# A hybrid decoder layer on one core: the scheduler's other model of the engines puts the same program in order

## The chip, the cores and the metric

The kernel runs on one core of a Trainium2 chip. The metric is the device time of one execution in microseconds (us), as the median of several runs. The engines of the core are TensorE (PE in the profile, its weight loads PEld), VectorE (DVE), ScalarE (ACT), GpSimd (POOL) and SyncE (SP, which only issues DMAs here).

## The reference

One decoder layer on 512 tokens of width 1024, in float32 (cut to what matters):

```python
h = rms_norm(x, ln_mix_g)
q_a, kv_a, gate_a, q_b, k_b, v_b, r_b, alpha_b, merge = split(h @ w_in)
o_nsa = nsa_attention(...)   # 8 heads, 2 key heads: compressed, selected and window attention, gated
o_gla = gla(...)             # 4 heads of chunked gated linear attention, chunks of 64
mix = sigmoid(merge_1) * (o_nsa @ w_branch_nsa) + sigmoid(merge_2) * (o_gla @ w_branch_gla)
x = x + mix @ w_out
x = x + memory_cross_attention(rms_norm(x, ln_x_g), rms_norm(mem, ln_mem_g), ...)  # 256 memory tokens
x = x + conv_ffn(rms_norm(x, ln_ffn_g), w_up, conv_w, conv_b, w_down)              # width 2816
out = rms_norm(x, ln_final_g)
```

## The kernel before

**Arithmetic.** Activations lie transposed: 128 channels on the partitions, 512 tokens along the row. Every matrix product is made of three fast matmuls (`mm3`, L160 to L162; `dense_tok`, L197 to L199), because each operand is split in a high and a low part: ACT copies the high part (`wh`, L140), and DVE or POOL subtracts it from the raw value to get the low part (`wl`, L141; `lo_engine` says which of the two, and it is POOL during the attention stage).

**Weights.** All weights come as 141 blocks of 128x1024 float32 in the order in which the program takes them (`take`). SP loads a block into one of three `raw` buffers (L126), ACT and DVE or POOL split it into one of three `wh` and `wl` buffers, two blocks ahead of use. A dense product (`dense8`) uses up one block in 24 matmuls.

**Stages.** After a first stage of projections comes the sparse attention (names that begin with `nsa`): eight steps, two key heads times four blocks of 128 queries. In a step `nsa_scores` multiplies on PE (L562 to L594, into the three `sc` banks), DVE masks and takes maxima (L584, L596), ACT exponentiates (L612), DVE, ACT and POOL scale, and DVE weights the compressed part (L627); then `nsa_values` transposes on PE (L650, into the two `pt` banks), ACT and DVE split the result (L165, L166), PE multiplies with the values into the one `o` bank (L644), and ACT and DVE take that out (L664, L669). The gated linear attention follows (`gla`), in which L746 and L791 make states and scores, L791 to L823 outputs and L833 a sum of squares. Between these steps the program holds independent dense products (`fillers`, names with `fill`), whose place is written by hand:

```python
NSA_FILL = (2, 1, 2, 1, 1, 2, 0, 0)
...
    for kv in range(2):
        for i in range(4):
            cur = nsa_scores(kv, i)
            if prev is not None:
                nsa_values(*prev)
            prev = cur
            fill(NSA_FILL[kv * 4 + i])
```

After that come the merge, the output projection, the cross-attention, the up and down projections of the feed-forward part, and a tail that norms the last rows and stores them.

**What sets the order.** The program text fixes which engine runs each instruction, but not the final order on it. When the `tile.TileContext` closes, the Tile library plays the whole program against a model of the engines. Whenever an engine of that model can take an instruction, it gets, among its instructions whose inputs are finished and whose buffers are free, the one that was written first. What comes out is the fixed order of every engine's instructions (the queue of SP among them), the buffer that each tile gets, and with both the waits on semaphores. On the chip each engine then works through its list in that order and waits at the head of it.

## Time and profile before

| | |
|---|---|
| median of 3 runs | 873.84 us (873.72 to 873.98) |
| the profiled execution, device time | 875.57 us |
| its span, first to last instruction | 873.5 us |
| PE busy | 853.2 us, 98% of the span, 4174 matmuls |
| DVE, ACT, POOL busy | 557.7, 419.1, 214.2 us |
| DMA | 83.58 MB, 96 GB/s in the mean |

The span is what the views of the trace divide up; 2.1 us of the device time lie outside it. Matmuls overlap one another in the records, so a record is longer than the distance to the next one's start, and PE can be busy and still not be at its pace. Bracketed times in a timeline row are the idle time of that engine just before the instruction, with what ended it.

### The profile page before, as it was taken

The numbers are of one execution on the slowest core, as the hardware profiler recorded it, in microseconds if no ns is written. First come the engines' busy times: TensorE is split into PE (matmuls) and PEld (weight loads), VectorE is DVE, ScalarE is ACT, GpSimd is POOL, SyncE is SP. The second block draws the span as 40 slices with busy tenths as digits, with TensorE's granted clock in tenths as the row PEclk, the third lists the DMA queues.
The fourth block names the chain that finished last, engine by engine and source line by source line (L and its number), as shares of the span: only waits on it lengthen the run. The fifth ranks groups of instructions, "written<-read, shape, count | busy, mean of one in ns | idle before, by whom it ended". The sixth has DMA issues, their size and how long they took to land.

```text
span 873.5 us, 11086 instructions
## 1 busy us (share of the span) xinstructions
PE 853.2 (98%) x4174; PEld 708.0 (81%) x4174; DVE 557.7 (64%) x908; ACT 419.1 (48%) x731; POOL 214.2 (25%) x160
## 2 busy tenths in 40 slices
PE   9999989999998999999999999999999999999996
PEld 6987777777786878898888788888888888888996
DVE  7576977998858378454487669665533465565324
ACT  7466767798445455344446535433311233334311
POOL 1373444344333314112300222111100111112121
PEclk9999999999999999999999999999999999999999
DMA  8333221002221232244341132322222223222302
GB/s 293 116 123 97 73 73 49 25 2 73 67 78 49 96 116 103 96 169 146 123 143 49 48 121 74 120 96 97 97 97 96 97 86 108 90 97 102 121 25 97
DMA packets 26406, 83.58 MB, mean 96 GB/s; under 512 B 3056, under 2 KB 5104, under 8 KB 26352
## 3 DMA queue, kind: packets, MB, share of 16 engines
q1 hardware_dynamic: 26064, 82.58, 27.2%
q8 instruction: 33, 0.54, 0.3%
q10 hardware_dynamic: 288, 0.28, 0.1%
q14 instruction: 21, 0.17, 0.1%
HBM read 80.76 MB, written 2.10 MB: 95 GB/s over the span
## 4 chain that ended last, share of the span: by engine, by line
PE 88%; DVE 7%; ACT 3%; issue 1%; POOL 1%; ACTq 0%; POOLq 0%
PE up_ps_sc L161 4%; PE up_ps_sc L160 4%; PE up_ps_sc L162 4%; PE fill_ps_acc L160 3%; PE fill_ps_acc L161 3%; PE fill_ps_acc L162 3%; PE up_ps_pt L160 3%; PE up_ps_pt L161 3%; PE up_ps_pt L162 3%; PE up_ps_acc L161 2%; PE up_ps_acc L160 2%; PE up_ps_acc L162 2%; PE nsa_ps_o L644 2%; PE down_ps_sc L162 2%; PE nsa_ps_pt L650 2%; PE down_ps_sc L161 2%
## 5 line engine op out<-in xcount | busy, mean ns | idle before, releaser
L1068 POOL TENSOR_TENSOR up_s<-up_s,up_s 128x512 f32<-128x512 f32 x22 | 35.8, 1630 | 259.6 <-ACT up_wh L140 207.7
L140 ACT ACTIVATE up_wh<-up_raw 128x1024 fp32r<-128x1024 f32 x40 | 42.5, 1062 | 64.9 <-PE up_ps_sc L161 33.0
L141 DVE TENSOR_TENSOR up_wl<-up_raw,up_wh 128x1024 fp32r<-128x1024 f32 x40 | 62.8, 1569 | 16.0 <-ACT up_wh L140 15.9
L141 POOL TENSOR_TENSOR fill_wl<-fill_raw,fill_wh 128x1024 fp32r<-128x1024 f32 x16 | 38.5, 2407 | 48.7 <-ACT fill_wh L140 46.7
L160 PE MATMUL up_ps_sc<-xo_g,up_wh 128*128 128x512 f32 x124 | 48.7, 393 | 0.0
L162 PE MATMUL up_ps_sc<-xo_g,up_wl 128*128 128x512 f32 x124 | 48.3, 389 | 0.0
L161 PE MATMUL up_ps_sc<-xo_g,up_wh 128*128 128x512 f32 x124 | 48.3, 389 | 0.0
L160 PE MATMUL up_ps_pt<-xo_g,up_wh 128*128 128x512 f32 x104 | 40.6, 390 | 0.0
L162 PE MATMUL up_ps_pt<-xo_g,up_wl 128*128 128x512 f32 x104 | 40.5, 389 | 0.0
L161 PE MATMUL up_ps_pt<-xo_g,up_wh 128*128 128x512 f32 x104 | 40.5, 389 | 0.0
L612 ACT ACTIVATE nsa_s<-nsa_s,nsa_nm 128x128 f32<-128x128 f32 (+3 forms) x64 | 34.2, 536 | 11.7 <-DVE nsa_nm L603 11.7
L160 PE MATMUL fill_ps_acc<-in_g,fill_wh 128*128 128x512 f32 x96 | 38.3, 399 | 0.2 <-DVE fill_t L529 0.2
L161 PE MATMUL fill_ps_acc<-in_g,fill_wh 128*128 128x512 f32 x96 | 38.3, 399 | 0.0
L162 PE MATMUL fill_ps_acc<-in_g,fill_wl 128*128 128x512 f32 x96 | 38.1, 396 | 0.0
L162 PE MATMUL up_ps_acc<-xo_g,up_wl 128*128 128x512 f32 x88 | 34.2, 389 | 0.0
L161 PE MATMUL up_ps_acc<-xo_g,up_wh 128*128 128x512 f32 x88 | 34.2, 389 | 0.0
L160 PE MATMUL up_ps_acc<-xo_g,up_wh 128*128 128x512 f32 x88 | 34.2, 389 | 0.0
L1064 ACT ACTIVATE up_s<-up_s 128x512 f32<-128x512 f32 x22 | 13.8, 632 | 40.2 <-DVE up_s L1062 40.2
L140 ACT ACTIVATE down_wh<-down_raw 128x1024 fp32r<-128x1024 f32 x9 | 9.5, 1061 | 39.4 <-PE down_ps_sc L161 17.5
L224 POOL TENSOR_TENSOR xo_g<-xo_g,xo_t 128x512 f32<-128x512 f32 x7 | 12.3, 1756 | 63.8 <-ACT xo_g L214 61.3
L140 ACT ACTIVATE fill_wh<-fill_raw 128x1024 fp32r<-128x1024 f32 x16 | 16.9, 1057 | 21.9 <-PE fill_ps_acc L161 14.9
L160 PEld LDWEIGHTS up_ps_sc<-xo_g,up_wh 128*128 128x128 f32 x124 | 23.3, 188 | 5.1 <-issue 0.2
(943 smaller groups left out, 2716.0 us busy)
## 6 DMA issues: line engine op xcount, KB each, us to landing
up_raw<-in_w SPq DMA_DIRECT2D x44, 512.0 KB, 3.2
fill_raw<-in_w SPq DMA_DIRECT2D x20, 512.0 KB, 3.2
down_raw<-in_w SPq DMA_DIRECT2D x18, 512.0 KB, 3.2
proj_raw<-in_w SPq DMA_DIRECT2D x14, 512.0 KB, 3.3
mix_raw<-in_w SPq DMA_DIRECT2D x12, 512.0 KB, 3.3
mkv_raw<-in_w SPq DMA_DIRECT2D x8, 512.0 KB, 3.2
wout_raw<-in_w SPq DMA_DIRECT2D x8, 512.0 KB, 3.4
in_s<-in_xT SPq DMA_DIRECT2D x8, 256.0 KB, 5.4
```

The costliest lines, as they stand in the source:

```text
L140: nc.scalar.activation(wh[:, c], r[:, c], AF.Copy)
L141: lo.tensor_tensor(wl[:, c], r[:, c], wh[:, c].bitcast(F32), op=ALU.subtract)
L160: nc.tensor.matmul(ps, w[0], x[0], start=first, stop=False)
L161: nc.tensor.matmul(ps, w[0], x[1], start=False, stop=False)
L162: nc.tensor.matmul(ps, w[1], x[0], start=False, stop=last)
L224: eng.tensor_tensor(state[0], state[0], q, op=ALU.add)
L612: nc.scalar.activation(s[:, :w], s[:, :w], AF.Exp, scale=sl, bias=nm[:, c:c + 1], accum_out=sums[:, c:c + 1])
L644: nc.tensor.matmul(po, v, x, start=j == 0 and x is parts[0], stop=j == last and x is parts[-1])
L650: nc.tensor.transpose(pt[:, g * P:(g + 1) * P], srcs[g], C("ident"))
L1064: nc.scalar.activation(cv, cv, AF.Gelu_apprx_tanh)
L1068: nc.gpsimd.tensor_tensor(gm, gm, cv, op=ALU.mult)
```

## The change

One argument is added where the context is opened. It tells the library to play the program against its other model of the engines, a simulation of the whole timeline, when it chooses the order. No instruction is added, taken away or given to another engine by the text of the kernel, and no size, buffer count or hand-written place of a filler changes. What can change is the order of the instructions on each engine and in each DMA queue, which buffer a tile gets, and which waits follow from both.

```diff
-    with tile.TileContext(nc) as tc:
+    with tile.TileContext(nc, schedule_with_timeline_sim=True) as tc:
         layer_kernel(tc, *args, order)
```

## Rows read from the trace of the kernel before

**Rows 1.** The page, busy time of each engine (share of the span, instructions).

```profile
PE 853.2 (98%) x4174; PEld 708.0 (81%) x4174; DVE 557.7 (64%) x908; ACT 419.1 (48%) x731; POOL 214.2 (25%) x160
```

**Rows 2.** Busy time in five stretches: length, engines (instructions), PE clock, DMA share, GB/s.

```profile
40.00:78.00 38.00, 36.76 (x245) 30.60 (x243) 26.72 (x46) 23.08 (x33) 24.62 (x18) 1.00 0.42 139
78.00:222.00 144.00, 136.68 (x691) 107.94 (x691) 118.90 (x337) 108.78 (x267) 60.85 (x52) 0.99 0.14 48
222.00:310.00 88.00, 85.01 (x428) 69.34 (x428) 60.53 (x100) 40.27 (x67) 28.02 (x13) 1.00 0.20 67
310.00:820.00 510.00, 509.88 (x2346) 425.28 (x2347) 306.03 (x360) 206.91 (x296) 80.56 (x51) 1.00 0.31 106
820.00:873.50 53.50, 46.16 (x274) 43.45 (x272) 19.71 (x29) 12.88 (x28) 12.49 (x11) 0.97 0.14 50
```

**Rows 3.** PE's waits, the first of the list: total us, times, longest.

```profile
PE nsa_ps_o L644 <- DVE nsa_t L669: 3.2, 4, 1.9
```

**Rows 4.** Timeline of PE around its six longest waits.

```profile
78.41 0.60 PE L562 MATMUL nsa_ps_sc<-proj_kcmp,proj_g 128*128 128x62 f32 x4 [1.12 <-DVE nsa_mx L596]
78.84 0.47 PE L160 MATMUL fill_ps_acc<-in_g,proj_wh 128*128 128x512 f32 x1
...
111.06 0.47 PE L644 MATMUL nsa_ps_o<-nsa_pth,proj_g 128*128 128x512 f32 x1 [1.92 <-DVE nsa_t L669]
111.37 0.40 PE L162 MATMUL fill_ps_acc<-in_g,fill_wl 128*128 128x512 f32 x1
111.60 0.40 PE L160 MATMUL fill_ps_acc<-in_g,fill_wh 128*128 128x512 f32 x1
...
170.53 0.44 PE L581 MATMUL nsa_ps_sc<-in_pair,proj_g 128*128 128x384 f32 x1 [0.91 <-DVE nsa_mx L584]
...
171.69 0.39 PE L197 MATMUL gla_ps_acc<-fill_wh,in_g 128*128 128x512 f32 x1
...
210.41 0.47 PE L644 MATMUL nsa_ps_o<-nsa_pth,proj_g 128*128 128x512 f32 x1 [0.98 <-ACT gla_s L202]
210.72 0.39 PE L197 MATMUL gla_ps_sc<-gla_wh,in_g 128*128 128x512 f32 x1
...
262.60 0.45 PE L160 MATMUL fill_ps_acc<-in_g,fill_wh 128*128 128x512 f32 x1
263.93 1.12 PE L833 MATMUL gla_ps_pt<-gla_t,in_cst 128*128 128x512 f32 x2 [0.88 <-ACT gla_t L828]
...
266.47 0.73 PE L746 MATMUL gla_ps_sc<-gla_s,gla_t 64*128 64x256 f32 x8 [0.98 <-DVE gla_t L166]
```

**Rows 5.** Timeline of DVE: five long instructions ahead of those waits.

```profile
73.89 2.40 DVE L316 TENSOR_TENSOR proj_g<-proj_t,proj_g 64x512 fp32r<-64x512 f32 x1
...
106.72 2.48 DVE L627 TENSOR_TENSOR proj_cm<-proj_cm,nsa_cf 128x124 f32<-128x124 f32 x1
...
168.37 1.26 DVE L501 COPY fill_dec<-fill_t 128x8 f32<-128x8 f32 x1
...
206.92 2.48 DVE L783 TENSOR_TENSOR gla_g<-fill_g,gla_g 64x512 fp32r<-64x512 f32 x1
...
263.38 2.43 DVE L166 TENSOR_TENSOR gla_g<-gla_t,gla_g 128x512 fp32r<-128x512 f32 x1 [0.41 <-ACT gla_g L165]
```

**Rows 6.** Line L627, all eight: shortest, median and longest in ns.

```profile
L627 DVE TENSOR_TENSOR proj_cm<-proj_cm,nsa_cf x8: 268/273/2475, 86.0 to 202.8; 128x124 f32<-128x124 f32 x8
```

**Rows 7.** Timeline of POOL at the second of them.

```profile
106.63 2.43 POOL L141 TENSOR_TENSOR fill_wl<-fill_raw,fill_wh 128x1024 fp32r<-128x1024 f32 x1
```

**Rows 8.** Busy time in two short stretches around 111 us, columns as in rows 2.

```profile
107.00:110.50 3.50, 2.14 (x11) 1.48 (x10) 3.49 (x7) 1.18 (x3) 2.05 (x1) 1.00 0.12 20
...
112.40:115.90 3.50, 3.50 (x12) 2.81 (x11) 2.18 (x6) 2.74 (x10) 0.39 (x1) 0.51 0.02 5
```

**Rows 9.** PE's matmuls that read `in_g`, 200 to 222.1 us: length, busy (count), clock, DMA.

```profile
200.00:222.10 22.10, 9.99 (x37) 1.00 0.21 74
```

**Rows 10.** Timeline of DVE in the tail.

```profile
857.82 4.88 DVE L1150 SCALAR_TENSOR_TENSOR wout_g<-wout_g,in_sm,down_rstd 128x384 f32<-128x384 f32 x6
```

## The prediction, made before the changed kernel was run

> **What bounds the kernel now.** I read the busy times on the page first: PE is busy for 853.2 us, 98% of the span of 873.5 us [rows 1], so at most some 20 us of the span are idle on the engine that carries the work, and an order that is only an order cannot win more than part of that. The second view is the busy time by stage [rows 2]. The reader is to see where those 20 us lie. From 310 to 820 us PE is busy for 509.88 of 510 us: there is nothing to win there, only something to lose. From 820 to the end 7.3 us are idle, nearly all of it behind the last matmul. From 78 to 222 us, the sparse attention, 7.3 of 144 us are idle, from 222 to 310, the linear attention, 3.0 of 88, and 1.2 of 38 before them. So the change is decided between 40 and 310 us, over 11.5 us of idle PE. DVE is busy for 118.90 of those 144 us and ACT for 108.78: they have slack, but not much, and the chain from scores to probabilities to values runs through both.
>
> The third view is the list of PE's waits, and then the timeline around each. The waits are short and many, none over 1.92 us, and they end on DVE most often, above all at the release of the single `o` bank (3.2 us in four waits) [rows 3]. The six longest are 1.12, 1.92, 0.91, 0.98, 0.88 and 0.98 us, 6.79 together [rows 4]. What the reader is to see in them is the row behind the wait. At 78.41 PE stands for 1.12 us before the compressed scores, and right behind these comes a filler matmul at 78.84 that needs nothing new: the block of weights it belongs to is half used, and it runs without a wait. At 111.06 it is the same, with the rest of a started block at 111.37. At 210.41 the next matmul of the value projection follows at 210.72. At 170.53 the value projection goes on at 171.69, behind the scores that were waited for. Ahead of the waits at 263.93 and 266.47 a filler block had been begun at 262.60, with a single matmul of its 24. So in all six PE stood before an instruction that was not ready while one that was stood in line behind it. The order was made by a model in which the first was ready: a greedy choice does not put an unready instruction ahead of a ready one.
>
> **The change part by part.** Nothing is added or removed, so there is no new instruction to cost; what is moved is the places of instructions in five lists, and which buffers they use. I cost it by what each place can be worth.
>
> *The six waits.* If the other model times DVE and ACT in this stretch as the chip does, it issues fillers where PE now stands. A filler takes 0.23 us from start to start (111.37 to 111.60) [rows 4], so the waiting instruction then starts at most that much late. Gain: from 0 to 6.79 us.
>
> *The clock.* After the wait of 1.92 us PE's granted clock is 0.51 for the 3.5 us from 112.40 to 115.90, that is about the lower of its two levels, 1.2 in place of 2.4 GHz; just before, from 107.00, PE was busy for only 2.14 of 3.50 us [rows 8]. All 3.5 us are busy, so at the full level the same work would take some 1.8 us and 1.7 us would be saved. This goes together with the wait at 111.06. Gain: from 0 to 1.7 us.
>
> *The start and the saturated part.* All 141 blocks are taken in the same order, and each is loaded and split two blocks ahead. I put the change from 310 to 820 us at zero, since 0.12 us of idle PE in 510 [rows 2] leave nothing to win; what hides every reordering of DVE, ACT and POOL there is their load, 306.03, 206.91 and 80.56 us of 510. If this cover failed for one block, PE would stand for about the splitting of that block, which at POOL's 2.43 us [rows 7] is the upper bound that I have for a single miss. SP's queue also carries the loads of the memory tokens and of the residual stream, which wait for a free buffer and could stand ahead of weights; with the blocks two ahead I take nothing for it.
>
> *The tail.* Behind the last matmul stands a fixed chain. Ahead of it DVE does six scalings of finished rows, 4.88 us in one go [rows 10]. They end at 862.70, 10.8 us before the span's end. If the new order puts them later, up to 4.9 us are lost; if earlier, nothing is won. I take zero.
>
> *Sum.* Between 0 and 6.79 + 1.7 = 8.5 us are to be had, and the trace has no row that says how well the other model knows the engines. I choose the middle, 4.2 us, because the two halves of the evidence point apart. For the gain: the waits all have ready work behind them. Against it: five of the six come behind a DVE instruction that took far longer than its size explains. L627 works on 128x124 elements; its eight instances have a median of 273 ns, but the one at 106.72 took 2.48 us [rows 5, 6]. POOL began a subtraction of a weight block at 106.63 that took 2.43 us [rows 7], and the two ended 0.14 us apart. So that DVE instruction stood still until POOL was done, and the wait at 111.06 is its consequence. The others are L316 at 73.89, L501 at 168.37, L783 at 206.92 and L166 at 263.38, 1.26 to 2.48 us each [rows 5]. A model that misses this will place the next such collision as blindly as the old one.
>
> The Trainium skill has this as a rule ("SBUF — State Buffer", section "Who interferes with whom"): a DVE instruction with two inputs in SBUF contends with a GpSimd instruction that reads SBUF, and the one that starts second is blocked for the whole of the first. The trace agrees, 2.48 us against 0.27. By that rule alone an order that leaves the subtractions on POOL meets as many collisions as before, and the sum would be zero and not 4.2 us.
>
> The sum against the profiled execution is 875.57 - 4.2 = 871.4 us of device time. That execution lies 1.73 us above the median of the runs shown, so for the median it is 873.84 - 4.2 = 869.6 us.
>
> **The rivals.** A measurement of this kernel can tell about 0.2%, or 1.75 us, from no change.
>
> *The collisions come again.* The new order moves the POOL subtractions against DVE's small instructions, some waits go and others of 1 to 2 us come. For it speaks that five of six waits hang on collisions [rows 4, 5]. Against it: a collision only costs PE when a waiting instruction stands ahead of ready work, and just that is what a better model would mend. Also in this rival is the case that both models choose nearly the same order, which the saturated 510 us make likely for most of the program. Time: 873.84 us, within 0.2%.
>
> *The fillers are used up too early (slower).* In the last two steps of the sparse attention the hand-written plan gives no fillers, and the cover is the matmuls of the value projection and the first product behind it: 37 matmuls that read `in_g` lie between 200 and 222.1 us, 9.99 of 22.1 us of PE's time in the records [rows 9]. If the new model lets PE take such work earlier, whenever it is ready for a moment, and puts attention instructions behind it, the chain through DVE and ACT ends no sooner and stands without cover at its end. At 0.23 us each, all 37 are worth 8.5 us, so 873.84 + 8.5 = 882.3 us. It decides from 18 matmuls on, where it outweighs the 4.2 us gained. For it speaks that even now, with the cover in place, a wait of 0.98 us lies in these 22 us [rows 4]. Against it speaks that more fillers stand behind (from 225 us on), though these are held back by the three buffers of split weights.
>
> *Something is put in the way at the end (slower).* The six scalings of the tail land among the last additions, or a load in SP's queue stands ahead of weights: up to 4.9 us, 878.7 us. Against it: in the old order the scalings end 10.8 us before the span does [rows 10], and PE waits for no load between 310 and 820 us [rows 2].
>
> **How the numbers follow.** Forecast, faster by about 4 us: 0.42. Collisions come again, or nothing moves: 0.18. Fillers used up early: 0.28. Tail or queue: 0.12. The last two are slower, 0.40 together. The best case, 873.84 - 8.5 = 865.3 us, and the worst, 882.3 + 4.9 = 887.2 us, bound the range; a little is cut off at either end: 866 to 886.5 us. The forecast's own range, from half its gain to all of the bound, is 866 to 872 us.
>
> **What would show it.** Right: PE's waits between 40 and 310 us add up to 4 to 8 us and not 11.5, those of more than 0.8 us with ready fillers behind them are gone, the clock stays at its upper level through 116 us, and the value projection's matmuls still lie between the last attention steps. The long DVE instructions behind POOL are still there, as many or nearly. The collisions: as many waits as before, at other places, each behind a long DVE instruction. The fillers: the stretch from about 200 us to the end of the attention has fewer than 19 such matmuls, and PE is idle there for 4 us or more. The forecast would be wrong above all if the saturated part shows idle PE, or if the attention as a whole got longer while PE filled it.

## The result and the profile after

The change makes the kernel slower: 895.11 us in the median of four runs (894.47 to 896.52), against 873.91 us for the kernel before beside it, a ratio of 1.0242 (1.0224 to 1.026), or 21.2 us. The profiled execution has a span of 892.5 us against 873.5.

First the page's busy line, then the stretches of [rows 2] (the columns are those given there).

```profile
PE 859.1 (96%) x4174; PEld 713.4 (80%) x4174; DVE 562.4 (63%) x908; ACT 419.2 (47%) x731; POOL 213.7 (24%) x160
```

```profile
40.00:78.00 38.00, 38.00 (x248) 32.16 (x247) 30.98 (x54) 21.26 (x30) 26.90 (x18) 1.00 0.41 139
78.00:222.00 144.00, 123.96 (x585) 95.15 (x584) 105.44 (x305) 97.33 (x247) 54.14 (x48) 0.93 0.10 34
222.00:310.00 88.00, 84.02 (x429) 67.95 (x430) 64.64 (x110) 43.48 (x76) 28.31 (x16) 0.98 0.21 72
310.00:820.00 510.00, 509.04 (x2332) 423.14 (x2331) 305.49 (x359) 209.02 (x298) 82.83 (x53) 1.00 0.29 103
820.00:892.50 72.50, 65.46 (x385) 63.14 (x383) 29.68 (x44) 20.75 (x41) 14.19 (x12) 0.98 0.25 88
```

The span grew by 19.0 us. TensorE's (PE's) busy time grew by 859.1 - 853.2 = 5.9 us with the same 4174 matmuls, its idle time by the other 13.1. The idle time lies in the attention. From 78 to 222 us PE is idle for 20.0 us where it was for 7.3 [rows 2], it gets through 585 matmuls where it got through 691, and the granted clock is 0.93 where it was 0.99. The stretch ahead is better than before (no idle time in 38 us, 1.2 before), the saturated one practically unchanged (0.96 us idle in 510), and the tail has 7.0 us against 7.3. Where the 5.9 us of busy time lie can't be read from these stretches, since they don't hold the same work.

PE's list of waits (us in all, times, longest) stands against [rows 3]:

```profile
PE nsa_ps_o L644 <- DVE nsa_ptl L166: 7.1, 4, 5.9
PE nsa_ps_sc L581 <- DVE nsa_mx L584: 5.6, 8, 2.5
PE nsa_ps_o L644 <- DVE nsa_t L669: 2.0, 3, 0.9
```

The longest wait is 5.9 us where it had been 1.9. The timeline of PE shows what surrounds that longest one, in the place of [rows 4]; the two rows behind it are of VectorE (DVE) and GpSimd (POOL) in the same microseconds.

```profile
100.86 0.39 PE L162 MATMUL fill_ps_acc<-in_g,fill_wl 128*128 128x512 f32 x1
101.09 1.04 PE L650 MATMUL nsa_ps_pt<-in_cst,nsa_s 128*128 128x128 f32 x8
...
105.85 0.44 PE L581 MATMUL nsa_ps_sc<-in_pair,proj_g 128*128 128x384 f32 x1 [1.34 <-DVE nsa_mx L584]
...
115.56 0.80 PE L644 MATMUL nsa_ps_o<-nsa_ptl,proj_g 128*128 128x512 f32 x1 [5.95 <-DVE nsa_ptl L166]
...
125.50 0.50 PE L160 MATMUL fill_ps_acc<-in_g,fill_wh 128*128 128x512 f32 x1 [0.87 <-DVE fill_t L529]
```

```profile
107.00 7.25 DVE L431 TENSOR_TENSOR_SCAN fill_g<-in_cst,fill_t 128x64 f32<-128x64 f32 x16
...
114.83 0.68 DVE L166 TENSOR_TENSOR nsa_ptl<-nsa_ps_pt,nsa_pth 128x512 fp32r<-128x512 f32 x1
```

```profile
107.42 4.67 POOL L141 TENSOR_TENSOR fill_wl<-fill_raw,fill_wh 128x1024 fp32r<-128x1024 f32 x2 [8.92 <-ACT fill_wh L140]
```

Two things are to be seen. Between the filler matmul at 100.86 and the next at 125.50 there is none: for 24.5 us no filler covers the attention's waits. And on VectorE the 16 scans of the gated attention's decay, a filler's work, stand ahead of the split that the value product waits for, and are stretched from 3 to 7.25 us by two of GpSimd's subtractions. So there are two theories.

**Theory 1, the cover is used too early.** The busy times of PE on the tile `fill_ps_acc` alone, up to the first compressed scores (L562) and up to the first value product (L644), first of the kernel before, then of the changed one:

```profile
0.00:78.40 78.40, 3.36 (x12) 2.11 (x12) 0.00 (x0) 1.00 0.50 175
0.00:95.10 95.10, 14.48 (x57) 10.26 (x57) 1.37 (x2) 1.00 0.44 152
```

```profile
0.00:87.40 87.40, 15.28 (x64) 11.73 (x64) 0.69 (x1) 1.00 0.46 163
0.00:108.80 108.80, 23.53 (x96) 17.64 (x96) 1.37 (x2) 0.99 0.40 141
```

64 filler matmuls stand ahead of the first scores where 12 stood, and 96 ahead of the first value product where 57 stood (102 and 63 with the six small ones of the decay). The attention starts later with them: the first scores at 87.4 us in place of 78.4, the first value product at 108.8 in place of 95.1, while PE has no idle time from 40 us to the first scores. **Theory 2, VectorE's queue:** what stands ahead of the split is the cause, wherever the fillers are.

### The profile page after: what moved, and what is told of

It reads as the page before. It is cut to its first block, busy times and chain, and to the rows that moved or that the text cites. A ratio compares the mean times of both kernels' runs of the same rounds, so it can differ in the third digit from the quotient of the medians.

```text
span 892.5 us, 11096 instructions
## 1 busy us (share of the span) xinstructions
PE 859.1 (96%) x4174; PEld 713.4 (80%) x4174; DVE 562.4 (63%) x908; ACT 419.2 (47%) x731; POOL 213.7 (24%) x160
## 4 chain that ended last, share of the span: by engine, by line
PE 87%; DVE 7%; ACT 5%; issue 1%; DMA 0%; POOL 0%; ACTq 0%; DVEq 0%
PE fill_ps_acc L160 4%; PE fill_ps_acc L161 4%; PE fill_ps_acc L162 4%; PE up_ps_sc L161 3%; PE up_ps_sc L160 3%; PE up_ps_sc L162 3%; PE up_ps_pt L161 3%; PE up_ps_pt L162 3%; PE up_ps_pt L160 3%; PE up_ps_acc L161 2%; PE up_ps_acc L160 2%; PE up_ps_acc L162 2%; ACT nsa_s L612 2%; PE nsa_ps_o L644 2%; PE down_ps_sc L162 2%; PE down_ps_sc L161 2%
## 5 line engine op out<-in xcount | busy, mean ns | idle before, releaser
L165 ACT ACTIVATE nsa_pth<-nsa_ps_pt 128x512 fp32r<-128x512 f32 x38 | 22.2, 594 | 12.0 <-PE nsa_ps_pt L650 11.6
L584 DVE CUSTOM_DVE_ANT_0 nsa_s<-nsa_ps_sc,in_cst 128x128 f32<-128x128 f32 (+3 forms) x32 | 15.5, 484 | 19.2 <-PE nsa_ps_pt L650 15.4
```

The costliest lines, as they stand in the source:

```text
L165: nc.scalar.activation(h, src, AF.Copy)
L584: nc.vector.tensor_tensor_reduce(out=s[:, :n], in0=ps[:, :n], in1=C("slc")[:, 384 - P * i:512], op0=ALU.add, op1=ALU.max, scale=1.0, scala ...
```

## The experiments

Most runs hold an engine to an order that one of the two kernels has, or to one made up of both. The kernel's text stays as it is, and behind it each instruction is tied to the one that shall stand ahead of it on its engine:

```diff
         layer_kernel(tc, *args, order)
+        for engine, places in PINNED.items():
+            seq = [written[engine][p] for p in places]
+            for ahead, behind in zip(seq, seq[1:]):
+                tc.add_manual_dep(behind, ahead.name, NO_SYNC)  # order on the engine only
```

| run | order on the engines | us | ratio to before |
|---|---|---|---|
| e1 | all changed, held in the old model | 896.71 | 1.026 (1.0244 to 1.0275) |
| e2 | changed to 101 us, then before's | 885.61 | 1.0135 (1.012 to 1.015) |
| e3 | changed to 130 us, then before's | 884.93 | 1.013 (1.0113 to 1.0147) |
| e4 | changed, scans behind the split | 895.35 | 1.0245 (1.0229 to 1.026) |
| e5 | before's to 127 us, then changed | 888.22 | 1.0157 (1.0142 to 1.0172) |
| e6 | PE before's, others by the other model | 906.31 | 1.0369 (1.0351 to 1.0386) |
| e7 | changed to 72 us, then before's | 874.30 | 0.9994 (0.9985 to 1.0003) |
| e8 | changed to 87 us, then before's | 881.62 | 1.0084 (1.0067 to 1.0102) |
| e9 | PE by the other model, others before's | 923.71 | 1.0552 (1.053 to 1.0574) |
| e10 | PE as in e8, others by the old model | 893.67 | 1.0222 (1.0193 to 1.0251) |
| e11 | before's, six waits covered on PE | 877.57 | 1.0035 (1.0024 to 1.0046) |
| e12 | PE changed, others by the old model | 919.52 | 1.0508 (1.0485 to 1.0531) |
| e13 | other model, fillers held back | 903.77 | 1.0336 (1.0322 to 1.035) |
| e14 | old model, fillers held back | 909.52 | 1.0406 (1.039 to 1.0422) |
| e15 | changed to 193 us, then before's | 890.76 | 1.019 (1.0176 to 1.0204) |
| e16 | before's, two waits covered on PE | 873.75 | 1.0001 (0.9992 to 1.001) |
| e17 | old model, fillers 1 each step | 883.72 | 1.0109 (1.0081 to 1.0137) |
| e18 | other model, fillers 1 each step | 896.21 | 1.0253 (1.0236 to 1.027) |

The kernel before took 874.0 to 874.3 us beside each of them.

### Is it the order at all, and where is the time lost (e1, e2, e3, e5, e15)

```diff
-PINNED = {}
+PINNED = {e: changed[e] for e in ENGINES}                              # e1
+PINNED = {e: upto(changed[e], 101.2) + rest(before[e]) for e in ...}   # e2; e3: 130.4, e15: 193.0
+PINNED = {e: upto(before[e], 127.4) + rest(changed[e]) for e in ...}   # e5
```

> The kernel before with its own model, but every engine held, instruction by instruction, to the order that the other model gave (buffer slots and semaphores are still handed out by the old one). Theory 1 and its rivals alike need order to be the whole of it: 895 us, within 2. If what counts is something else that the switch changes (slots, semaphores), the time falls towards 874 and the rest of the study is about that.

> The changed order up to 101 us of its own trace, and from there on all that is left in the order of before. By then the changed order has issued 102 to 111 filler matmuls where before had issued 63 at the same step of the attention. Theory 1 (cover used too early): the order behind 101 us is the old one, but its fillers are already gone, so the waits that they covered come out: 882 us or more. Theory 2 (VectorE's queue: the 16 scans and a collision with GpSimd stand ahead of the split that the attention waits for) has its cause behind 101 us, which is the old order here: 877 us or less.

> The changed order up to 130 us of its own trace, then what is left in the order of before. The excess of TensorE's time over its pace up to there is about 12 us above before. Theory 1 with local losses: 874 + 12 = 886 us, and the 9 us lost between 180 and 260 us are a matter of the order there. If those later losses follow from the early ones (fillers gone), they come here too: 893 to 896 us.

> The mirror of the cut at 130 us: the order of before up to the third value product (127 us of its trace, 126 filler matmuls issued in both orders at that step), then what is left in the changed order. If the losses behind 180 us are made by the order there: 874 + 10 = 884 to 886 us. If they only follow from what the changed order did earlier: 874 to 877 us.

> The changed order up to 193 us of its own trace (the sixth value product), then what is left in the order of before. The cut at 130 us gave 884.9 us, the whole changed order 896.7 held in the same way. Theory 1: TensorE went without cover from 181 to 193 us while 18 matmuls of the value projection had been issued before: 884.9 + 7 = 892 us here, and 4 to 5 us are left for the stretch behind. If all of the late loss lies behind 193 us: 885 us.

The order is the whole of it: held in the old model, it takes 896.7 us, 1.6 us more than the changed kernel. The loss has several places. What stands ahead of 101 us costs 11.6 us (e2), although everything behind is in the old order. From 101 to 130 us nothing is added (e3, 10.9 us). Up to 193 us it is 16.8 us (e15), up to the end 22.7 (e1). The late part alone costs 13.9 us (e5), 2 us more than I had expected, so that the parts on either side of 130 us add up to 24.8, a little more than the whole.

e2 shows the mechanism best. Here are the windows from the first transposed probabilities to the same point behind the next step's, all engines first, then `fill_ps_acc` alone; the first pair is of the kernel before, the second of e2.

```profile
91.10:116.80 25.70, 23.23 (x110) 18.45 (x109) 22.62 (x77) 19.11 (x47) 7.91 (x8) 0.93 0.20 71
91.10:116.80 25.70, 13.72 (x48) 9.40 (x49) 0.69 (x1) 0.93 0.20 71
```

```profile
101.10:126.60 25.50, 13.52 (x51) 10.19 (x50) 19.52 (x58) 15.38 (x35) 4.99 (x5) 0.70 0.12 42
101.10:126.60 25.50, 0.57 (x2) 0.44 (x2) 0.69 (x1) 0.70 0.12 42
```

The same stretch of the attention takes 25.7 us with 48 filler matmuls in it and 25.5 us with two. The order on VectorE and ScalarE is before's in both, and their work sets the length: in the chain of work that ended last, from ScalarE's part of a filler's decay (L424) to the end of the window, 17.2 us are VectorE's and ScalarE's in the kernel before and 17.7 in e2. The first 7.2 us of it are in both that decay itself, so the chain isn't the attention's alone. Used up ahead, the fillers bring the attention no sooner to its end, and their 0.23 us each [rows 4] come on top: by this count 39 of them are 9.0 of the 11.6 us.

That the two lengths agree so closely is in part luck. Of the attention's own score matmuls (`nsa_ps_sc`) e2 has 12 in its window and before 25, since e2 had run the rest ahead. And before's profile holds the 3.5 us at the lower clock of [rows 8], which isn't in every execution (see the clock, below): in e16, whose order is before's up to 165 us and whose clock stays at 1.00 there, 23.8 us lie between the start of the first transposition and the next filler behind the last (90.91 to 114.75), in before 25.4 (91.11 to 116.53), in e2 25.1 (101.14 to 126.23). In e2 the granted clock is 0.70 in the window, and PE, with 12.0 us idle, has 7.4 us of matmuls in the chain, nearly all at the lower level; at the upper one they would take about half of it, so by my estimate up to 3.7 us of e2's window are the clock's.

The later places look alike. Three windows of the changed kernel, then the same of e3, where the order is before's there:

```profile
181.00:193.00 12.00, 8.74 (x37) 4.97 (x35) 10.50 (x40) 11.55 (x40) 3.31 (x5) 0.99 0.00 1
200.00:207.00 7.00, 4.52 (x19) 3.53 (x18) 6.76 (x18) 1.86 (x4) 0.48 (x1) 0.76 0.01 2
240.00:260.00 20.00, 16.78 (x89) 12.91 (x88) 14.88 (x31) 11.83 (x24) 3.46 (x4) 0.94 0.15 52
```

```profile
181.00:193.00 12.00, 11.95 (x64) 9.46 (x63) 10.90 (x35) 9.28 (x28) 4.74 (x5) 1.00 0.00 1
200.00:207.00 7.00, 7.00 (x39) 5.83 (x38) 6.94 (x15) 6.81 (x18) 3.21 (x3) 1.00 0.01 4
240.00:260.00 20.00, 20.00 (x101) 16.93 (x100) 14.98 (x23) 9.50 (x18) 8.91 (x4) 1.00 0.23 80
```

PE's matmuls that read `in_g`, that is the fillers and the value projection, in the first two windows, first of the changed kernel, then of e3:

```profile
181.00:193.00 12.00, 0.00 (x0) 0.99 0.00 1
200.00:207.00 7.00, 0.00 (x0) 0.76 0.01 2
```

```profile
181.00:193.00 12.00, 6.29 (x22) 1.00 0.00 1
200.00:207.00 7.00, 5.11 (x19) 1.00 0.01 4
```

The changed order leaves PE idle for 3.3, 2.5 and 3.2 us in three windows in which before's order, after the same start, leaves it idle for 0.05 us in all, and in the first two it has none of this cover where e3 has 41 matmuls. The third shows less: in e3 the sparse attention is over by then (last value product at 229.26 us, in the changed kernel at 253.83). VectorE is busy for about as long in both (32.1 and 32.8 us in all three).

### How much of the cover must be gone (e7, e8)

```diff
+PINNED = {e: upto(changed[e], 72.1) + rest(before[e]) for e in ...}    # e7; e8: 87.5
```

> The changed order up to 72 us only (2 filler matmuls issued), then the order of before. TensorE's excess over its pace up to there is 0.69 us in the changed order and 2.22 us in that of before, and the wait of 1.12 us before the first compressed scores may be met later or not: 871 to 873 us, faster than before by 0.1 to 0.3 per cent. A slower time would mean that a part of the loss lies in the first 72 us.

> The changed order up to 87.5 us, where the first compressed scores start: 64 filler matmuls are issued, in the order of before 12 at this step. Behind it the order of before. Theory 1: 52 matmuls of cover (12 us of TensorE) are used up already here, so a large part of the 11.6 us of the cut at 101 us shows: 878 to 884 us. If the loss is made by the orders of the other engines between 87 and 101 us, it doesn't show: 871 to 874 us.

With 2 filler matmuls ahead of their old place nothing is lost, with 52 at the first scores 7.3 us, with 39 still ahead at the first value product (e2) 11.6. It isn't the number alone. In e8 no filler runs between the first scores and the first value product (101.67 us, 6.5 us later than before), which has 64 ahead of it where before has 57: most of the 7.3 us have come up by there, in a stretch without cover, and 52 times 0.23 us would be 12.0. From 91.9 to 98.9 us of it the granted clock is 0.53. The small gain expected of the first 72 us isn't there: 874.30 against 874.32. In the profile the wait before the first scores has gone down from 1.12 to 0.78 us, but 0.55 us of wait have come up at 73.81 in the preparation ahead of it.

### VectorE's queue (e4)

```diff
-    DVE: ..., 16 scans (L431), L532, L616, split (L166), ...
+    DVE: ..., L616, split (L166), ..., scale of the maxima (L603), 16 scans (L431), L532, ...
```

> The changed order with one edit on VectorE: the 16 scans of the decay and the product that follows them stand behind the scale of the row maxima that ran at 119.6 us, not ahead of the split at 114.8 us. Theory 2 (VectorE's queue is the cause): the wait of 5.9 us at 115.6 us shrinks to under 1 us and 5 to 7 us come back: 888 to 890 us. Theory 1 (no cover left): the wait moves to the next step of the attention, and the time stays at 892 us or above.

Against e1 it gives 1.4 us, not 5 to 7. The scans themselves are short now (258 ns in the median, none over 417), and the wait of 5.95 us is gone. The timeline of PE in e4 shows what came in its place:

```profile
109.03 0.80 PE L644 MATMUL nsa_ps_o<-nsa_pth,proj_g 128*128 128x512 f32 x1 [1.07 <-ACT nsa_pth L165]
...
119.83 0.79 PE L581 MATMUL nsa_ps_sc<-in_pair,proj_g 128*128 128x512 f32 x1 [3.63 <-DVE nsa_mx L584]
```

The work that was taken out of the way of one step stands in the way of the next. At this place theory 2 accounts for 1.4 of 22 us; no run changes VectorE's order throughout and nothing else.

### One engine's order without the others' (e6, e9, e10, e12)

```diff
+PINNED = {"PE": before["PE"]}                        # e6, other model
+PINNED = {e: before[e] for e in ENGINES if e != "PE"}  # e9, other model
+PINNED = {"PE": upto(changed["PE"], 87.5) + rest(before["PE"])}  # e10, old model
+PINNED = {"PE": changed["PE"]}                       # e12, old model
```

> The changed kernel (the other model), with TensorE alone held to its order of before; VectorE, ScalarE, GpSimd and the DMA queue are ordered by the other model around it. Theory 1 (the fillers' places on TensorE make the loss): 872 to 877 us. Theory 2 (the order on VectorE makes it, whatever TensorE does): 885 us or above. In between: both.

> The mirror of the run in which TensorE alone kept its old order: the other model orders TensorE, and VectorE, ScalarE, GpSimd and the DMA queue are held to their order of before. It again puts fillers ahead: 52 filler matmuls before the first compressed scores (before 12, changed 64) and 101 before the first value product (63 and 102). Theory 1 (the fillers' places on TensorE are enough for the loss): 885 us or above. Theory 3 (after the run with TensorE's old order at 906 us: the orders of the other engines make the loss, TensorE's only goes with them): 872 to 878 us.

> The kernel before and its model, with TensorE alone held to the order of the cut at 87 us (64 filler matmuls before the first compressed scores, then the order of before); the other engines are ordered around it by the model of before. Theory 1: about the 881.6 us of that cut, 879 to 884. Theory 3: the other engines are back to an order that suits, 872 to 876 us.

> The kernel before and its model, with TensorE alone held to the whole changed order; the other engines are ordered around it by the model of before. Theory 1: 890 us or above, TensorE's order alone carries the 21 us. Theory 3: well below 885 us.

After e6 I had added a theory 3: the orders of the other engines make the loss, and PE's only goes with them. No one of the three theories fits all four runs: by the ranges that I had set, e6 came out as theory 2 has it, e9 and e12 as theory 1, e10 as none. Three of the four are slower than the changed kernel itself, so they measure something else as well. PE's old order did not bring the time back (e6, 906.3), the others' old orders did not either (e9, 923.7), and under the model of before the cut at 87 us costs 893.7 us when the other engines are ordered around it anew (e10), 12 us more than when they keep the order that belongs to it (e8). The first two rows of PE's waits in e6, then in e9, then in e12 (us in all, times, longest):

```profile
PE nsa_ps_o L644 <- ACT nsa_pth L165: 13.5, 5, 4.5
PE nsa_ps_o L644 <- DVE nsa_ptl L166: 3.2, 3, 1.5
```

```profile
PE nsa_ps_o L644 <- DVE nsa_ptl L166: 8.0, 7, 4.4
PE gla_ps_o L823 <- DVE gla_s L166: 4.2, 2, 2.5
```

```profile
PE nsa_ps_sc L593 <- DVE nsa_mx L596: 9.6, 6, 3.1
PE nsa_ps_sc L581 <- DVE nsa_mx L584: 6.1, 4, 4.1
```

The longest waits in these rows are 4.5, 4.4 and 4.1 us (e12 has one of 4.9 before a filler), each before a step whose copy, split or maximum another engine finishes late. So the order of one engine said little by itself here. e6 and e9 say nothing on where the loss of the changed kernel comes from; they say that five lists must suit each other, and that a list made around another engine's fixed one, by either model, was 12 to 50 us worse here than the list that belonged to it.

### The waits of the forecast, covered by hand (e11, e16)

```diff
-    PE: ..., wait + L562, fill x12, ...          (78.41, and so at 111.06, 170.53, 210.41, 263.93, 266.47)
+    PE: ..., fill x6, L562, fill x6, ...         (e11: all six, 5 to 9 matmuls each; e16: those at 170.53 and 210.41)
```

> No other model: the order of before on all engines, with one edit on TensorE. Ahead of each of the six waits that the prediction counted (6.8 us in all) stand the 5 to 9 filler or value projection matmuls that ran next behind it, 35 in all, so that each wait of 0.9 to 1.9 us is covered. If these waits can be had for nothing, as the prediction's sum has it: 866 to 868 us. If each only moves to the next step, or its cover is missed later: 872 to 875 us. The prediction's half: 869.6.

> The order of before on all engines with two of the six edits alone: ahead of the waits of 0.91 us (170.5 us) and 0.98 us (210.4 us) stand the five value projection matmuls that ran next behind each. In the run with all six edits nothing longer than 0.5 us had come up near these two. If a covered wait is a gain where no other wait takes its place: 1.9 us less, 872 to 872.5 us. If cover is only moved: 873.5 to 874.5 us.

With all six covered the kernel is slower, by 3.4 us. The new waits of e11, and VectorE and GpSimd ahead of the first of them:

```profile
PE nsa_ps_sc L578 <- DVE proj_cm L565: 3.5, 1, 3.5
PE nsa_ps_o L644 <- DVE nsa_ptl L166: 2.8, 5, 1.7
PE gla_ps_sc L746 <- DVE gla_t L795: 2.2, 2, 2.0
```

```profile
L421 DVE SCALAR_TENSOR_TENSOR fill_raw<-fill_t x2: 2666/2747/2828, 87.4 to 89.9; 128x512 f32<-128x512 f32 x2
```

```profile
87.07 2.40 POOL L141 TENSOR_TENSOR fill_wl<-proj_raw,fill_wh 128x1024 fp32r<-128x1024 f32 x1
89.80 2.43 POOL L141 TENSOR_TENSOR fill_wl<-fill_raw,fill_wh 128x1024 fp32r<-128x1024 f32 x1 [0.32 <-ACT fill_wh L140]
```

Six fillers moved by one step shifted L421 and GpSimd's subtractions so that both instances of L421 now meet one, 2.67 and 2.83 us in place of 1.62 and 0.68 before. That is the rival of the prediction in which the collisions come again, and it takes more than the covered wait of 1.12 us gave. In e16, which touches no such place, PE's idle time from 165 to 222 us went down from 3.25 to 1.64 us, and still only 0.3 us of 1.9 came through, which can't be told from nothing. (The two profiled executions, 873.61 and 875.57 us, lie 1.96 us apart, but about 1.7 of it are the clock stretch of [rows 8], which e16's doesn't have.) So a covered wait was worth little here even where no collision took its place.

### Held back, and other fillers (e13, e14, e17, e18)

```diff
             if fillers:
...
+                # first PE instruction of the filler behind the last one written ahead of it
+                tc.add_manual_dep(first, ahead.name, NO_SYNC)                  # e13, e14
```

```diff
-NSA_FILL = (2, 1, 2, 1, 1, 2, 0, 0)
+NSA_FILL = (1, 1, 1, 1, 1, 1, 1, 1)                                            # e17, e18
```

> The changed kernel with the fillers held back: the first matmul of each filler on TensorE may not stand ahead of the last TensorE instruction that is written before it. 0 filler matmuls now stand before the first compressed scores and 54 before the first value product (changed 64 and 102, before 12 and 63); all else is left to the other model. Theory 1 (fillers too early): most of the loss goes, 875 to 883 us. Theory 3 (the other model suits this chip badly on all engines, wherever the fillers stand): 890 us or above.

> The control: the same holding back in the kernel before, with its own model (4 filler matmuls before the first compressed scores, 54 before the first value product, against 12 and 63). If holding back costs or gives little by itself: 872 to 878 us. What it gives or costs here is to be taken off the run with the other model.

> The kernel before with one line changed: one filler is written behind each of the eight attention steps, in place of 2, 1, 2, 1, 1, 2, 0, 0. 12 filler matmuls stand before the first compressed scores and 41 before the first value product (before 12 and 63). If the places in the source set how well the cover meets the waits, this is slower than before, 876 to 890 us.

> The same line in the changed kernel: 64 filler matmuls before the first compressed scores and 78 before the first value product (changed 64 and 102). If the other model has a price of its own, it is some 21 us behind the same source under the old model. If the price is that of this source's fillers under it, the distance is another one, under 12 us, and may turn round: 880 to 892 us.

Holding the fillers back repairs nothing: 903.8 us under the other model, and the control shows that it costs 35.5 us under the old one. The likely reason is that it holds them too strictly, so that cover comes too late; no run shows it. But beside its control the other model is here 5.75 us ahead. With one filler behind each step it is 12.5 us behind, which is just over what I had allowed, at a time that is also above my range. From 5.75 us ahead to 21.2 behind, with the same engines and the same work: the price isn't a fixed one of the model, it depends on the source under this model. e13 by itself came out as its theory 3 has it, but against its control e14 it disproves that the other model suits the chip badly wherever the fillers stand.

## Why the prediction was wrong

The step that failed is the sum: "Between 0 and 6.79 + 1.7 = 8.5 us are to be had", of which I took the middle. Covering all six waits by hand cost 3.4 us (e11), covering two gave 0.3 (e16). Its lower bound failed with it: that the other model would issue fillers "where PE now stands" was a condition for the gain, and the sum has no term for fillers issued at other places. The changed order issues them ahead of the attention, and the part of it ahead of 101 us alone costs 11.6 us (e2). The idle times of single waits were added up as if the work that covers them came from nowhere. It is taken from the next place that it covers, and in this stretch VectorE and ScalarE set the pace: with and without 48 fillers, 25.7 and 25.5 us. A smaller slip: the six waits aren't the six longest between 40 and 310 us, for PE waits 0.94 us before a filler at 280.99; the six longest add up to 6.85 us.

The mechanism of the result was among the rivals, at 0.28, as "the fillers are used up too early", and its place and its size were off. I looked for it in the last two steps, where 37 matmuls are worth 8.5 us. It begins far ahead of them: 52 fillers too many are gone by the first scores and 39 by the first value product, and PE is without any from 101 to 125.5 us (11.6 us by e2). From 181 us on, cover is missing again in places (another 11.1, e1 less e2, of which 5.95 lie behind 193 us, e1 less e15). At the place that I had named it is not: from 200 us to the end of the sparse attention (254.4 us) the changed kernel has 108 matmuls that read `in_g`, not fewer than 19. PE is idle there for 6.1 us, over the 4 that I had named, but for only 1.3 of it in the last two steps (from 228.8 us). The rival had the mechanism, but its sign on the cover would have missed it. What I didn't weigh is that fillers can run from 70 us on, as they do in the changed kernel, well before the attention, and that running them then looks like a gain: PE has no idle time from 40 to 78 us.

*The clock:* I had it as a gain of up to 1.7 us that goes with the wait at 111.06. That was misread. e16 meets the same wait in the order of before, and its clock stays at the upper level:

```profile
110.86 0.47 PE L644 MATMUL nsa_ps_o<-nsa_pth,proj_g 128*128 128x512 f32 x1 [1.92 <-DVE nsa_t L669]
```

```profile
112.40:115.90 3.50, 3.50 (x21) 2.92 (x20) 1.98 (x4) 2.94 (x10) 0.39 (x1) 1.00 0.02 5
```

There, as in e7, the wait is met without the fall, so the 3.5 us at the lower level don't follow from the wait alone. The profiled execution of the kernel before lies 1.73 us above the median, which is about the 1.7 us of the term: very likely the median had that gain already, and the sum took it off once more. In the changed kernel the clock went the other way, 0.93 against 0.99 from 78 to 222 us. That is likely a part of the 5.9 us more of busy time, as matmuls are that stand alone and count with their whole records; no run tells the two apart.

*The collisions:* expected as many as before. They came at other places, with 4.2 us on the scans alone, and taking those away gave 1.4 us (e4). They make the longest new wait of e11; in the changed kernel this one is a small part.

*310 to 820 us and the tail at zero:* right, 0.96 against 0.12 us idle and 7.0 against 7.3.

*What stays open:* why this model lets the fillers go first and the other doesn't, and how much of the 11.6 us of e2 is the clock's (up to 3.7 in its window, by the estimate above). That PE's place of the fillers by itself makes the loss was to be tried by e9, e10 and e12, and couldn't be, since each brought new orders of the other engines with it. What is shown is that the part of the order ahead of 101 us, with PE's fillers and the other engines' lists together, makes 11.6 us of the loss, that the part behind makes the rest, and that cover is missing in both.

## What to carry to other kernels

Where independent work fills the gaps of a latency chain, ask what sets the chain's length. If it takes about the same time with and without the fillers, a filler that runs before the chain begins gains nothing: the chain starts later and then stands uncovered. A list of waits with ready work behind each is no sum of gains, for the work that covers one can be missing at the next. A stretch at the lower clock in one profiled execution is worth a look at a second profile before it is counted as a term. And the orders of several engines are one thing: judge a scheduler by the whole program it makes of your source, measured, and not by one engine's list.

## What the runs showed of the hardware

A short VectorE instruction can take nine times its usual time beside GpSimd: two of the 16 scans on 128x64 elements took 2.38 us, the median 0.26, while GpSimd did two subtractions of 2.3 us each. The scan reads two inputs in SBUF, and so it agrees with the rule of the Trainium skill that the prediction cites ("SBUF — State Buffer", section "Who interferes with whom"), by which the instruction that starts second is blocked for the whole of the first.

```profile
L431 DVE TENSOR_TENSOR_SCAN fill_g<-in_cst,fill_t x16: 260/262/2377, 107.0 to 114.0; 128x64 f32<-128x64 f32 x16
```

Such collisions hang on fractions of a microsecond. In e11 L421 began 0.68 us earlier than before and GpSimd's second subtraction 1.04 us earlier (89.80 in place of 90.84), and L421 went from 2.30 us for both instances to 5.49.

The granted clock fell behind the same wait in one execution and not in others. After the wait of 1.92 us before L644, with before's order around it, it was 0.51 for 3.5 us in the profiled execution of the kernel before, and 1.00 in those of e7 and e16.
